# One matmul of 512 tokens per weight tile, instead of two of 256, in the first phase of a convolution and RWKV-7 block

## The chip, the cores and the metric

The kernel runs on one core of a Trainium2 chip. The core has five engines, each with its own queue of instructions that it works off in order: TensorE (PE; its weight loads are listed apart as PEld), VectorE (DVE), ScalarE (ACT), GpSimd (POOL) and SyncE (SP), which issues the DMAs. An instruction may wait for semaphores that other engines or DMAs raise. The metric is the device time of one execution in microseconds (us), the median of three runs.

## The reference, cut to what matters

One layer, 2048 tokens, 1024 channels, float32. A normalised and modulated input `h` goes through one combined projection; a convolution branch and an RWKV-7 branch use its parts, and their merged output goes through further projections.

```python
h = _rmsnorm(x, norm_g[l]) * (1.0 + scale[:, None, :]) + shift[:, None, :]
p = jnp.einsum('bsd,de->bse', h, w_in[l])
c_val, c_gate, c_og, ts, r_og, g_conv, g_rwkv = jnp.split(p, SPLITS, axis=-1)
y_conv = _conv_branch(c_val, c_gate, c_og, conv_k[l], conv_b[l], conv_ln_g[l], conv_ln_b[l], w_conv_out[l])
y_rwkv = _rwkv7_branch(ts, r_og, ...)
m = jax.nn.sigmoid(g_conv) * y_conv + jax.nn.sigmoid(g_rwkv) * y_rwkv
out = jnp.einsum('bsd,de->bse', m, w_out[l])
x = x + gate[:, None, :] * out
...
def step(state, inp):
    r_t, w_t, k_t, v_t, kk_t, b_t = inp
    sk = jnp.einsum('bhvk,bhk->bhv', state, kk_t)
    state = (state * w_t[:, :, None, :] - sk[..., None] * b_t[:, :, None, :]
             + v_t[..., None] * k_t[:, :, None, :])
    return state, jnp.einsum('bhvk,bhk->bhv', state, r_t)
```

The projection has 9344 output columns, 73 tiles of 128 channels. The recurrence (`step`) is serial in the tokens.

## The kernel before

The 2048 tokens are cut into four blocks of 512 (`TB`). The **first phase** makes, for each block, the 73 projection tiles, the convolution and the recurrence, and leaves its results in memory; the **second phase** makes the output projections (tiles `co` and `ro`, then `pout`) and the final norm.

A projection tile (`mm3k`, lines 183 to 193) is a sum over 8 blocks of depth and three products: weights and inputs are split into a high and a low part (`w_hi`, `w_lo`, `h_hi`, `h_lo`) in a rounded 32-bit format, and high x high, high x low and low x high are added in one PSUM tile. Each product is `ms` matmuls over 512 / `ms` tokens; `ms` is `MS` in the first phase and `MS2` in the second. The PSUM tiles `ps_main` come from the pool `pm` with two buffers (line 234), so a projection cannot begin before the last reader of the one two before it is done.

The recurrence runs for 16 heads in four **groups** of two pairs of heads (`group`, `pair`). Before a group can run, each of its pairs needs its projections of k, r and v (`shifted`, lines 410 to 424: ScalarE scales the tile, VectorE adds the previous token's share at L420 and L422, and the small copy at L424 writes `carry`, which is the tile's last reader), the decay (matmuls L452 to L458 with the small weights `wl`, then eight running sums on VectorE at L463, one for each chunk of 64 tokens), head sums (L490), products of keys and queries (L522, masked on VectorE at L524), transposes (L537, L553), and a triangular inversion on GpSimd (L591, L593) with transfers on both sides. Then eight **chunks** follow, each a chain: TensorE L665 and L670, VectorE copies X (L673), TensorE L679, VectorE makes uv (L681), TensorE L685, VectorE updates the state S (L690), and the next chunk's L665 reads S. L650 gives the previous chunk's output. After the last chunk come the group's statistics (L707 to L716) and transposes (L721).

The convolution has 31 taps of 512 tokens on VectorE (L756), 0.75 us each. The projections of the convolution and of the gates (`project`, L730) depend on nothing in the recurrence, so they can stand anywhere between its links.

The order of the instructions in each engine's queue is not the order of the code. A scheduler orders the program when it is built, by its own estimate of how long each instruction takes and by priorities (`high_priority` puts a few ahead). At run time nothing is reordered between the engines' instructions: what stands first in a queue and waits holds up what is behind it.

Of the kernel before, what the change touches and what calls it, by code (L numbers as in the profile page):

```python
# [41 lines left out]
OE, LE, CE = 0, 0, 1  # L42
WLL = 1
TRE = 1
MS, MS2 = 2, 1
WB = 6
KEPT = ("in",)
def lplan(t):
# [1085 lines left out]
```

## Time and profile before

| | |
|---|---|
| median of 3 runs | 3144.74 us (3140.74 to 3146.39) |
| span of the profiled execution | 3131.2 us |
| TensorE's granted clock, mean over the span | 0.981 |
| matmuls of L192 with 256 columns | 4608 for each of the three products, 285 ns each |
| matmuls of L192 with 512 columns (second phase) | 192 or 128 a group of rows, 398 to 421 ns each |
| convolution taps (L756) on VectorE | 697.9 us busy |
| GpSimd's inversion (L591, L593) | 179.8 and 191.9 us busy |
| DMA | 638.42 MB, 204 GB/s over the span |

The profiled span is one execution, from its first instruction to its last, and lies 13.5 us under the median of the runs. Matmuls are pipelined: a row's duration is longer than the distance to the next one's start, and it is that distance which is the rate. In a timeline row stand the start, the duration, engine, line, operation, output and inputs, the shape, and how many instructions were merged; brackets give the idle time before and what ended it. A 32-bit matmul that is not in the rounded format is carried out as two, so four L665 rows in the trace are two in the program.

### The profile page before, as it was taken

The numbers are of one execution on the slowest core, as the hardware profiler recorded it, in microseconds if no ns is written. First come the engines' busy times: TensorE is split into PE (matmuls) and PEld (weight loads), VectorE is DVE, ScalarE is ACT, GpSimd is POOL, SyncE is SP. The second block draws the span as 40 slices with busy tenths as digits, with TensorE's granted clock in tenths as the row PEclk, the third lists the DMA queues.
The fourth block names the chain that finished last, engine by engine and source line by source line (L and its number), as shares of the span: only waits on it lengthen the run. The fifth ranks groups of instructions, "written<-read, shape, count | busy, mean of one in ns | idle before, by whom it ended". The sixth has DMA issues, their size and how long they took to land.

```text
span 3131.2 us, 64840 instructions
## 1 busy us (share of the span) xinstructions
PE 2990.4 (96%) x25672; PEld 2808.5 (90%) x25672; DVE 2169.9 (69%) x4326; ACT 1045.9 (33%) x1887; POOL 1125.1 (36%) x1692
## 2 busy tenths in 40 slices
PE   6799998999999999999999999999999999699998
PEld 5789998999999999999999999999999988487888
DVE  6686877676767665867667586758598455977643
ACT  4424333333323242423142324132332223343421
POOL 3354545424342424141313235326256014643100
PEclk9899999999999999999999999999999999899999
DMA  8665758563747476545546557636457657756554
GB/s 300 215 240 191 259 199 275 195 235 126 256 141 244 150 244 216 190 156 182 178 164 194 186 193 243 198 130 214 137 166 262 215 174 264 261 198 232 189 185 158
DMA packets 343328, 638.42 MB, mean 204 GB/s; under 512 B 133424, under 2 KB 152176, under 8 KB 343024
## 3 DMA queue, kind: packets, MB, share of 16 engines
q1 hardware_dynamic: 343024, 634.27, 60.4%
q8 instruction: 202, 3.31, 0.4%
q14 instruction: 102, 0.84, 0.1%
HBM read 462.10 MB, written 170.92 MB: 202 GB/s over the span
## 4 chain that ended last, share of the span: by engine, by line
PE 71%; DVE 10%; DMA 9%; POOL 4%; issue 2%; SPq 2%; ACT 2%; DVEq 0%; POOLq 0%; ACTq 0%
PE ps_main L192 50%; PE aux L522 3%; PE xo L679 2%; PE xo L650 2%; PE xo L670 2%; DMA w_st<-w_in_t 2%; PE xo L665 2%; PE xo L685 2%; PE pout L1055 1%; POOL TT L593 1%; PE pout L1056 1%; PE pout L1054 1%; POOL itmp L591 1%; DVE acc L756 1%; DMA w_gr<-grow_d 1%
## 5 line engine op out<-in xcount | busy, mean ns | idle before, releaser
L192 PE MATMUL ps_main<-h_hi,w_hi 128*128 128x256 f32 x4608 | 954.9, 285 | 23.1 <-ACT w_hi L175 19.7
L192 PE MATMUL ps_main<-h_hi,w_lo 128*128 128x256 f32 x4608 | 959.1, 285 | 8.1 <-POOL w_lo L177 6.6
L192 PE MATMUL ps_main<-h_lo,w_hi 128*128 128x256 f32 x4608 | 959.0, 285 | 0.0
L192 PEld LDWEIGHTS ps_main<-h_hi,w_hi 128*128 128x128 f32 x4608 | 718.8, 190 | 33.6 <-ACT w_hi L175 20.8
L192 PEld LDWEIGHTS ps_main<-h_hi,w_lo 128*128 128x128 f32 x4608 | 717.2, 189 | 17.9 <-POOL w_lo L177 8.2
L192 PEld LDWEIGHTS ps_main<-h_lo,w_hi 128*128 128x128 f32 x4608 | 717.7, 189 | 6.8 <-issue 0.5
L756 DVE SCALAR_TENSOR_TENSOR acc<-u,ck,acc 128x512 f32<-128x512 f32 x928 | 697.9, 752 | 20.4
L175 ACT CAST w_hi<-w_st 128x1024 fp32r<-128x1024 f32 x135 | 141.5, 1048 | 327.7 <-DMA w_st<-w_in_t 120.8
L591 POOL TENSOR_TENSOR itmp<-La,TT 128x126 f32<-128x126 f32 (+22 forms) x496 | 179.8, 363 | 137.4 <-DMA La<-dA 102.1
L690 DVE SCALAR_TENSOR_TENSOR S<-xo,pe,Se 64x64 f32<-64x64 f32 x512 | 144.8, 283 | 108.4 <-PE xo L685 99.1
L593 POOL TENSOR_TENSOR TT<-TT,itmp 128x126 f32<-128x126 f32 (+22 forms) x496 | 191.9, 387 | 36.0
L177 DVE TENSOR_TENSOR w_lo<-w_st,w_hi 128x1024 fp32r<-128x1024 f32 x88 | 117.8, 1339 | 110.0 <-PE ps_main L192 53.7
L660 ACT ACTIVATE Se<-S,pe 128x128 f32<-128x128 f32 x256 | 89.1, 394 | 232.7 <-DVE S L690 232.3
L177 POOL TENSOR_TENSOR w_lo<-w_st,w_hi 128x1024 fp32r<-128x1024 f32 x47 | 112.5, 2394 | 136.2 <-ACT w_hi L175 83.5
L545 POOL TENSOR_TENSOR vv<-rk,vv 128x512 f32<-128x512 f32 x32 | 43.2, 1350 | 324.4 <-ACT rk L544 324.4
L681 DVE TENSOR_TENSOR uv<-xo,rn 64x256 f32<-64x256 f32 x128 | 53.9, 421 | 129.7 <-PE xo L679 128.7
L522 PE MATMUL aux<-KR,BKz 128*128 128x128 f32 x1024 | 139.9, 282 | 2.8 <-DVE As L524 2.1
L522 PEld LDWEIGHTS aux<-KR,BKz 128*128 128x128 f32 x1024 | 126.2, 194 | 5.7 <-DVE As L524 2.4
L524 DVE TENSOR_TENSOR As<-aux,maskA 128x512 f32<-128x512 f32 x128 | 86.8, 687 | 52.8 <-PE aux L522 51.9
L673 DVE COPY X<-xo 64x256 f32<-64x256 f32 x128 | 53.6, 419 | 89.5 <-PE xo L670 88.6
L652 ACT COPY uv<-xo 64x256 f32<-64x256 f32 x128 | 46.8, 365 | 175.7 <-PE xo L650 175.2
L665 PE MATMUL xo<-S,KR 128*128 128x128 f32 x512 | 96.4, 280 | 6.9 <-DVE S L690 6.7
(294 smaller groups left out, 5464.1 us busy)
## 6 DMA issues: line engine op xcount, KB each, us to landing
w_hi<-kh_in SPq DMA_DIRECT2D x219, 512.0 KB, 3.8
w_lo<-kl_in SPq DMA_DIRECT2D x219, 512.0 KB, 4.9
w_st<-w_in_t SPq DMA_DIRECT2D x73, 512.0 KB, 4.4
kh_in<-w_hi SPq DMA_DIRECT2D x71, 512.0 KB, 2.9
kl_in<-w_lo SPq DMA_DIRECT2D x71, 512.0 KB, 4.3
w_st<-w_ro_t SPq DMA_DIRECT2D x32, 512.0 KB, 3.9
w_st<-w_co_t SPq DMA_DIRECT2D x32, 512.0 KB, 3.5
w_hi<-kh_o SPq DMA_DIRECT2D x32, 512.0 KB, 3.6
```

Source lines behind the costliest of these rows:

```text
L175: nc.scalar.copy(hi, st)
L177: lo_eng.tensor_tensor(out=lo, in0=st, in1=hi.bitcast(F32), op=ALU.subtract)
L192: nc.tensor.matmul(ps[:, qs], ww[:, k, :], aa[k][:, qs], start=(k == 0 and t == 0 and q == 0), stop=(k == KT - 1 and t == 2 and q == ms - ...
L522: nc.tensor.matmul(pA[:, c // 2, es], BKz[:, hh, cc, es], KR[:, cc, es], start=(c == 0), stop=(c == 3), skip_group_check=True)
L524: nc.vector.tensor_tensor(out=Asb[:, hh, c4 * 4:c4 * 4 + 4, :].rearrange("p (a e) n -> p a (e n)", e=2), in0=pA, in1=flat(maskA).unsqueeze ...
L591: nc.gpsimd.tensor_tensor(out=tmp[:, :ni, :nt], in0=La[:, j:j + 1, j + 1:].broadcast_to([P, ni, nt]), in1=TT[:, :ni, j:j + 1].broadcast_to ...
L593: nc.gpsimd.tensor_tensor(out=TT[:, :ni, j + 1:], in0=TT[:, :ni, j + 1:], in1=tmp[:, :ni, :nt], op=ALU.add)
L650: nc.tensor.matmul(xo[vr, q, hs], As[q][:, hh, c, rc], uv[:, c, q, hs], start=False, stop=(q == 1 and hh == 1), skip_group_check=True)
L660: nc.scalar.mul(Se[:, q, :], Sg[:, q, :], R[q]["pe"][:, c:c + 1])
L665: nc.tensor.matmul(xo[:, q, :], R[q]["KR"][:, cc, es], Sg[:, q, :], start=(q == 0), stop=False, skip_group_check=True)
L690: nc.vector.scalar_tensor_tensor(out=Sg[hs, q, hs], in0=xo[hs, 2 + q, hs], scalar=R[q]["pe"][hs, c:c + 1], in1=Se[hs, q, hs], op0=ALU.mult ...
L756: nc.vector.scalar_tensor_tensor(out=acc if i + 1 < HALO else yj, in0=u[:, i:i + TB], scalar=ck[:, j, i:i + 1], in1=acc, op0=ALU.mult, op1 ...
```

## The change

One constant: each product of a projection tile in the first phase is one matmul over all 512 tokens.

```diff
 TRE = 1
-MS, MS2 = 2, 1
+MS, MS2 = 1, 1
 WB = 6
```

In `mm3k` the loop over `q` then runs once, with all of `ps` and of the input tile. The first phase has 292 tiles (73 in four blocks), so 292 x 24 = 7008 pairs of matmuls become single ones, and as many weight loads go. No operation of another engine is added or removed. Since the scheduler orders the program anew, the change moves instructions on all engines. It does so most where one group of the recurrence ends and the next is prepared. The rows below are from the second block, where the second group (state `S_423`) ends and the third (`S_425`) begins.

On TensorE, before, at the last chunks of the group: the rows L192 are projections, two halves each, and between the last chunk's X and uv steps (L679) and those around it stand some ten of them.

```order
L192 MATMUL ps_main<-h_hi,w_lo 128x256 x2
L192 MATMUL ps_main<-h_hi,w_hi 128x256 x2
L192 MATMUL ps_main<-h_lo,w_hi 128x256 x2
L679 MATMUL xo<-X,As 64x64 x4
L665 MATMUL xo<-S_425,KR 128x128 x2
L670 MATMUL xo<-uv,As 64x64 x4
L192 MATMUL ps_main<-h_hi,w_lo 128x256 x2
L192 MATMUL ps_main<-h_hi,w_hi 128x256 x2
```

On TensorE, in the changed kernel, the same boundary:

```order
L192 MATMUL ps_main<-h_hi,w_lo 128x512
L679 MATMUL xo<-X,As 64x64 x4
L685 MATMUL xo<-uv,tk 128x128 x2
L665 MATMUL xo<-S_423,KR 128x128 x2
L670 MATMUL xo<-uv,As 64x64 x4
L650 MATMUL xo<-uv,As 64x64 x4
L679 MATMUL xo<-X,As 64x64 x4
L665 MATMUL xo<-S_425,KR 128x128 x2
L670 MATMUL xo<-uv,As 64x64 x4
L685 MATMUL xo<-uv,tk 128x128 x2
L452 MATMUL aux<-lw,wl 128x512
L453 MATMUL aux<-lw,wlo 128x512
```

Two chunks' links have no projection between them, and the next group's decay matmuls (L452 to L458) follow at once. The queue goes on, up to the next projection:

```order
L457 MATMUL aux<-la,wl 128x512
L458 MATMUL aux<-la,wlo 128x512
L650 MATMUL xo<-uv,As 64x64 x4
L490 MATMUL aux<-bones,sq 64x2 x8
L452 MATMUL aux<-lw,wl 128x512
L453 MATMUL aux<-lw,wlo 128x512
L457 MATMUL aux<-la,wl 128x512
L458 MATMUL aux<-la,wlo 128x512
L192 MATMUL ps_main<-h_hi,w_hi 128x512
```

Both pairs' decay matmuls now stand within a few rows of each other, with nothing of the projections around them; before, they stood further up and apart.

On VectorE, before, around the evacuation of the tiles r and v (L420 to L424) of the next group's second pair:

```order
L681 TENSOR_TENSOR uv<-xo,rn 64x256
L420 SCALAR_TENSOR_TENSOR r<-ps_main,v,t_12946 128x511
L422 SCALAR_TENSOR_TENSOR r<-carry,v,t_12946 128x1
L690 SCALAR_TENSOR_TENSOR S_423<-xo,pe,Se 64x64 x4
L424 COPY carry<-ps_main 128x1
L510 SCALAR_TENSOR_TENSOR rk<-r,hrk,ta 128x512
L420 SCALAR_TENSOR_TENSOR vv<-ps_main,v,t_13036 128x511
L422 SCALAR_TENSOR_TENSOR vv<-carry,v,t_13036 128x1
L673 COPY X<-xo 64x256
L424 COPY carry<-ps_main 128x1
```

On VectorE, in the changed kernel, between the last update of S_423 (with eight scans L463 right behind it) and the carry copy of the next group's first v tile:

```order
L493 TENSOR_SCALAR rn<-aux 128x8
L496 SCALAR_TENSOR_TENSOR y<-ta,k 128x512
L707 TENSOR_REDUCE gst<-uv 128x16
L494 RECIPROCAL rn<-rn 128x8
L483 SCALAR_TENSOR_TENSOR KR<-k,v,E_11274 128x4x64 x2
L497 SCALAR_TENSOR_TENSOR BK<-y,hkk,E_11277 128x4x128
L708 TENSOR_SCALAR gst<-gst 128x16
L463 SCALAR_TENSOR_TENSOR M<-one,M 128x64 x8
L510 SCALAR_TENSOR_TENSOR rk<-r,hrk,ta 128x512
L420 SCALAR_TENSOR_TENSOR vv<-ps_main,v,t_11466 128x511
L422 SCALAR_TENSOR_TENSOR vv<-carry,v,t_11466 128x1
L424 COPY carry<-ps_main 128x1
```

Before, the next group's tiles were evacuated between the links of the running recurrence; now the first v tile stands behind two sets of scans and the preparation of the pair, after the recurrence's end.

## The prediction

> **What bounds the kernel now.** First the page: the span, TensorE's share, the granted clock by slices, and the chain of work that ended last.
>
> ```profile
> span 3131.2 us, 64840 instructions
> PE 2990.4 (96%) x25672; PEld 2808.5 (90%) x25672; DVE 2169.9 (69%) x4326; ACT 1045.9 (33%) x1887; POOL 1125.1 (36%) x1692
> ...
> PE 71%; DVE 10%; DMA 9%; POOL 4%; issue 2%; SPq 2%; ACT 2%; DVEq 0%; POOLq 0%; ACTq 0%
> ```
>
> TensorE is busy 2990 of 3131 us and carries 71% of the chain, so the kernel runs at the rate at which matmuls stream, and the 141 us of idle are what is left of all waits. The question is what the change does to the rate, and what it does to the waits.
>
> Next the timeline of TensorE in a dense stretch of the first phase, where each row is two halves of one weight tile, and through one interruption:
>
> ```profile
> 800.12 0.40 PE L192 MATMUL ps_main<-h_lo,w_hi 128*128 128x256 f32 x2
> ...
> 804.83 0.40 PE L192 MATMUL ps_main<-h_hi,w_hi 128*128 128x256 f32 x2
> 805.07 0.60 PE L721 MATMUL late<-ident,uv 128*128 128x128 f32 x4
> 805.42 0.48 PE L192 MATMUL ps_main<-h_lo,w_hi 128*128 128x256 f32 x2
> 805.75 0.40 PE L192 MATMUL ps_main<-h_hi,w_lo 128*128 128x256 f32 x2
> ```
>
> From 800.12 to 804.83 there are 20 rows, so a pair takes 4.71 / 20 = 235.5 ns. The first pair after a small matmul takes 805.75 - 805.42 = 0.33 us, 0.095 more. The same at 512 columns, from the second phase, where the recurrence's last steps stand between projections:
>
> ```profile
> 2552.53 0.60 PE L665 MATMUL xo<-S,KR 128*128 128x128 f32 x4
> 2553.06 0.67 PE L670 MATMUL xo<-uv,As 64*64 64x64 f32 x8
> 2553.66 0.68 PE L650 MATMUL xo<-uv,As 128*64 128x64 f32 x8
> 2554.27 0.50 PE L192 MATMUL ps_main<-o_lo,w_hi 128*128 128x512 f32 x1
> ...
> 2556.01 0.40 PE L192 MATMUL ps_main<-o_lo,w_hi 128*128 128x512 f32 x1
> ...
> 2559.51 0.39 PE L192 MATMUL ps_main<-o_lo,w_hi 128*128 128x512 f32 x1
> 2559.83 0.68 PE L679 MATMUL xo<-X,As 64*64 64x64 f32 x8
> 2560.43 0.50 PE L192 MATMUL ps_main<-o_hi,w_lo 128*128 128x512 f32 x1
> 2560.77 0.39 PE L192 MATMUL ps_main<-o_lo,w_hi 128*128 128x512 f32 x1
> ...
> 2563.34 0.60 PE L685 MATMUL xo<-uv,tk 128*128 128x128 f32 x4
> 2563.70 0.48 PE L192 MATMUL ps_main<-o_hi,w_hi 128*128 128x512 f32 x1
> ```
>
> From 2556.01 to 2559.51 there are 15 matmuls: 233.3 ns each. After an interruption the first takes 0.34, again 0.1 more. The small matmuls of one chunk of the recurrence occupy TensorE for 0.53 + 0.60 + 0.61 (L665, L670, L650) + 0.60 (L679) + 0.36 (L685) = 2.70 us when projections stand between them.
>
> Such a chunk has a latency of its own, which shows once in the trace, where the order leaves its steps bare:
>
> ```profile
> 2486.86 0.60 PE L685 MATMUL xo<-uv,tk 128*128 128x128 f32 x4
> ...
> 2488.76 1.03 PE L665 MATMUL xo<-S,KR 128*128 128x128 f32 x4 [1.30 <-DVE S L690]
> ...
> 2491.52 1.11 PE L679 MATMUL xo<-X,As 64*64 64x64 f32 x8
> ...
> 2493.16 1.22 PE L685 MATMUL xo<-uv,tk 128*128 128x128 f32 x4 [0.52 <-DVE uv L681]
> ...
> 2495.46 0.63 PE L192 MATMUL ps_main<-o_hi,w_lo 128*128 128x512 f32 x1
> ...
> 2495.88 0.63 PE L192 MATMUL ps_main<-o_hi,w_hi 128*128 128x512 f32 x1
> ```
>
> From L685 to L685 it takes 6.30 us, 3.6 more than TensorE's own 2.70: the steps wait in turn for VectorE (S, X, uv). And behind it the projections come every 0.42 us instead of 0.233: the clock is granted at half.
>
> **The rate.** The change merges 7008 pairs (292 weight tiles of the first phase x 8 blocks of depth x 3 products). 7008 x (235.5 - 233.3 ns) = -15 us. The order has 701 entries into projections (or other 32-bit rounded matmuls) from small matmuls before, and 485 now: 216 x 0.095 = -20 us. Together -35 us, about 1%, and nothing hides them, since TensorE is the bound there.
>
> The Trainium skill ("TensorE: Matmul & The Clock Gate", section "Back-to-back issue gap") gives about 131 ns for a sustained matmul of 512 columns. By that a pair of 235.5 would become 131 and the change would bring -0.7 ms; the row at 233.3 ns, in this kernel with these operands, speaks against it.
>
> **The order.** This is where I expect the loss. The order is made anew, and at 13 of the 16 group boundaries TensorE's queue now has the recurrence's last steps bare, and behind them both pairs' decay matmuls (L452 to L458) of the next group, six rows apart; before, the two never stood closer than 24 rows, with projections between. Links of the recurrence (L665 to L679, L679 to L685, L685 to the next L665) with no projection in them: 4 before, 55 now (group boundaries, where another group's L665 stands in the link, counted as one link). That is about 4 for each of the 13 places, as in the place shown above. The projections that used to fill them are spent earlier, some 22 rows to a link where there were 12.
>
> What the next projection then waits for stands on VectorE. Both buffers of ps_main hold projections (v of the next group's first pair, k of its second), and the next one, r, needs the buffer that v's last reader, the carry copy at L424, gives back. VectorE has ahead of it what the last listing of the change shows (groups: busy us, mean ns of one, idle before):
>
> ```profile
> L463 DVE TENSOR_TENSOR_SCAN M<-one,M 128x64 f32<-128x64 f32 x256 | 82.7, 386 | 7.9 <-ACT M L455 7.4
> ...
> L510 DVE SCALAR_TENSOR_TENSOR rk<-r,hrk,ta 128x512 f32<-128x512 f32 x32 | 37.7, 1178 | 0.2
> ...
> L483 DVE SCALAR_TENSOR_TENSOR KR<-k,v,E 128x256 f32<-128x256 f32 x64 | 32.4, 515 | 0.2
> ...
> L497 DVE SCALAR_TENSOR_TENSOR BK<-y,hkk,E 128x512 f32<-128x512 f32 x32 | 27.8, 867 | 1.2
> ...
> L496 DVE SCALAR_TENSOR_TENSOR y<-ta,k 128x512 f32<-128x512 f32 x32 | 24.1, 755 | 0.0
> ...
> L420 DVE SCALAR_TENSOR_TENSOR vv<-ps_main,v,t 128x511 f32<-128x511 f32 x31 | 23.2, 747 | 29.6 <-ACT t L418 15.7 <-issue 8.2 <-POOL s_lo L271 3.5
> ...
> L707 DVE TENSOR_REDUCE gst<-uv 128x16 f32<-128x1024 f32 x16 | 19.5, 1220 | 6.0 <-ACT uv L652 5.6
> ```
>
> 16 scans x 0.386 + 0.755 (y) + 1.220 (gst) + 2 x 0.515 (KR) + 0.867 (BK) + 1.178 (rk) + 0.747 (vv) = 12.0 us, the small ones left out. None of it is new work, but before it was spread among the taps while TensorE had projections of its own.
>
> One place, from the last projection to the next: L679 to L685 1.64 (2493.16 - 2491.52); a bare chunk 6.30; S and on, 1.9 (2488.76 - 2486.86); VectorE 12.0: together 21.8 us. TensorE's own work in it is 0.60 + 0.36 + 2.70 + 8 decay matmuls x 0.233 = 5.5. So 16 us are lost, and 13 x 16 = **+210 us**. From below: if both sets of scans ran ahead, 6.2 less, and if only the bare links cost, 9.84 - 3.7 = 6 us, 13 x 6 = 78. From above, waits for ScalarE and GpSimd in the same row of steps, 20 us: 260. I take 210, since the scans need the decay matmuls, which stand behind the bare links on TensorE.
>
> After the next projections a second thin stretch follows in the order (L522, L721, L537, L553, L338 with hardly a projection), where VectorE's masks come ahead of the next evacuation:
>
> ```profile
> L524 DVE TENSOR_TENSOR As<-aux,maskA 128x512 f32<-128x512 f32 x128 | 86.8, 687 | 52.8 <-PE aux L522 51.9
> ```
>
> 4 x 0.687 = 2.7 us with TensorE's small matmuls running beside; between 0 and 6 us each I take 3, as the masks take: 13 x 3 = +39 us.
>
> **The clock.** The windows of two stretches (length, then busy us and instructions of TensorE's matmuls and weight loads, VectorE, ScalarE and GpSimd, then the granted clock, the DMA share and GB/s):
>
> ```profile
> 700.00:1000.00 300.00, 297.75 (x2826) 286.26 (x2825) 209.49 (x452) 96.02 (x184) 110.57 (x199) 1.00 0.59 193
> ...
> 2700.00:2800.00 100.00, 80.94 (x349) 63.82 (x350) 78.29 (x87) 39.25 (x54) 55.95 (x36) 0.88 0.59 197
> ```
>
> With TensorE filled the granted clock is 1.00; with 19 us idle in 100 it is 0.88, 12 us of clock. That is 0.63 us for a us of idle, or 10 us for one of the 13 places; the bare chunk above cost the projections behind it only six matmuls at 0.2 extra, 1.3. I take 5: 13 x 5 = +65 us (17 to 130). The Trainium skill ("TensorE: Matmul & The Clock Gate", section "What's actually happening") has it that an idle window of about 3.4 us halves the clock until a busy window has passed; an estimate by it is half of one to two windows, 1.7 to 3.4 us a place or 22 to 44 us, and the sum would be 3380 to 3402. The half-rate rows at 2495.46 agree with it in kind.
>
> **The sum.** 3131 - 35 + 210 + 39 + 65 = 3410 us for the span. The median of the runs, 3144.7, lies 13.5 above the profiled span, so 3424; I say **3420**. The work beside TensorE stays the same: VectorE, ScalarE, GpSimd and the DMAs do what they did, VectorE at 69%.
>
> **Rivals.**
> *The order does not bite, the rate decides* (faster): 3131 - 35 + 13.5 = 3110. For it: TensorE bounds at 96%, and in the stretch 700 to 1000 idles 2 us in 300. It decides if a place loses under 35 / 13 = 2.7 us; against it stands the bare chunk, which alone lost 3.6. 5%.
> *Only the bare links cost*, because VectorE has its scans behind it when TensorE comes: 3131 - 35 + 78 + 17 + 20 + 13.5 = 3225. 12%.
> *It bites harder*: 20 us a place, 6 in the second stretch, 10 of clock: 3131 - 35 + 13 x 36 + 13.5 = 3578. 6%.
> *The change does not do what it says*: it does, the order has 128x512 in phase one throughout; with loss and gain equal the time would stay within 0.2% (6 us, about what a measurement of this kernel can tell): 1%.
> My forecast holds 76%, 3330 to 3505 with the bounds of its terms. The range down to 3225 takes in half of the second rival. Faster 6%, same 2%, slower 92%.
>
> **What would show it.** Right: projections at 128x512 with 230 to 235 ns between starts; L424 (carry) as the releaser of L192's waits, some 100 us in all where it hardly shows now; about 13 stretches of 15 to 35 us with hardly a projection; a granted clock around 0.93 over the span; TensorE's share well below 96%; VectorE's busy time the same. Wrong: no such stretches and a span near 3100, then the steps ran ahead; or stretches ended by another releaser (a weight's DMA, GpSimd's inversion), then the place is right and the mechanism is not. If the projections themselves came faster than 230 ns, my rate is wrong.

## The result, and the profile after

| | median of 4 runs | lowest to highest | span of the profiled execution | TensorE's granted clock |
|---|---|---|---|---|
| before | 3142.74 us | 3137.01 to 3146.39 | 3131.2 us | 0.981 |
| after | 3418.11 us | 3403.50 to 3421.14 | 3415.8 us | 0.931 |

The ratio is 1.0869, with a 95% interval of 1.0844 to 1.0894: 273 us slower, and the forecast was 3420. Differences of medians below are ratios times 3142.7, since each set of runs has its own runs of before beside it.

The changed kernel's page, in the same order as before (span; busy time, share and instructions of each engine; the chain that ended last):

```profile
span 3415.8 us, 50909 instructions
...
PE 3056.6 (89%) x18664; PEld 2504.4 (73%) x18664; DVE 2239.0 (66%) x4326; ACT 1039.5 (30%) x1887; POOL 1125.2 (33%) x1692
...
PE   6899897989898989898989898989879999579998
...
PE 67%; DVE 13%; DMA 8%; POOL 4%; issue 4%; ACT 3%; SPq 1%; DVEq 0%; ACTq 0%; POOLq 0%
```

TensorE issues 7008 matmuls fewer and yet is busy 66 us longer, and idle for 359 us (3415.8 - 3056.6) where it was for 141. In the row of 40 slices (busy tenths of TensorE) nearly every other slice from the fifth on is an 8 or less: a hole that comes back with a period of two slices, some 170 us. What ends the holes is in the view of waits (TensorE's product, what it waited for; us in all, times, the longest) and in the group of the projections' first product (busy us, mean ns; idle before it), in the changed kernel and, below it, before:

```profile
PE ps_main L192 <- DVE carry L424: 143.4, 22, 11.2
```

```profile
L192 PE MATMUL ps_main<-h_hi,w_hi 128*128 128x512 f32 x2304 | 945.8, 411 | 159.2 <-DVE carry L424 143.4
```

```profile
L192 PE MATMUL ps_main<-h_hi,w_hi 128*128 128x256 f32 x4608 | 954.9, 285 | 23.1 <-ACT w_hi L175 19.7 <-DVE carry L424 2.5 <-DMA w_hi<-kh_in 0.5
```

One copy of 128 numbers on VectorE, 0.16 us long, releases 143 us of TensorE's waiting, where it released 2.5 us before. One of the holes in full, TensorE first (start, duration, instruction, idle before it and its releaser):

```profile
1043.24 0.39 PE L192 MATMUL ps_main<-h_hi,w_lo 128*128 128x512 f32 x1
1043.56 0.68 PE L679 MATMUL xo<-X,As 64*64 64x64 f32 x8
1044.75 0.71 PE L685 MATMUL xo<-uv,tk 128*128 128x128 f32 x4 [0.52 <-DVE uv L681]
1046.31 1.03 PE L665 MATMUL xo<-S,KR 128*128 128x128 f32 x4 [0.85 <-DVE S L690]
...
1050.34 0.71 PE L685 MATMUL xo<-uv,tk 128*128 128x128 f32 x4
1051.50 0.50 PE L452 MATMUL aux<-lw,wl 128*128 128x512 f32 x1 [0.45 <-ACT tk L554]
...
1056.65 0.63 PE L458 MATMUL aux<-la,wlo 128*128 128x512 f32 x1
1068.02 0.80 PE L192 MATMUL ps_main<-h_hi,w_hi 128*128 128x512 f32 x1 [10.74 <-DVE carry L424]
1068.61 0.63 PE L192 MATMUL ps_main<-h_lo,w_hi 128*128 128x512 f32 x1
```

From 1043.24 to 1068.02 TensorE has no projection. First the last links of the recurrence run bare, from 1043.56 to 1051; then the next group's decay matmuls, up to 1057; then nothing for 10.74 us. VectorE in the same hole:

```profile
1053.73 2.08 DVE L463 TENSOR_TENSOR_SCAN M<-one,M 128x64 f32<-128x64 f32 x8 [1.39 <-ACT M L455]
...
1057.76 1.92 DVE L483 SCALAR_TENSOR_TENSOR KR<-k,v,E 128x256 f32<-128x256 f32 x2
...
1060.60 4.51 DVE L463 TENSOR_TENSOR_SCAN M<-one,M 128x64 f32<-128x64 f32 x8
1065.03 0.72 DVE L510 SCALAR_TENSOR_TENSOR rk<-r,hrk,ta 128x512 f32<-128x512 f32 x1
1065.79 0.75 DVE L420 SCALAR_TENSOR_TENSOR vv<-ps_main,v,t 128x511 f32<-128x511 f32 x1
1066.45 1.32 DVE L422 SCALAR_TENSOR_TENSOR vv<-carry,v,t 128x1 f32<-128x1 f32 x1
1067.80 0.16 DVE L424 COPY carry<-ps_main 128x1 f32<-128x1 f32 x1
```

VectorE comes free of the recurrence when the decay values arrive (1053.73), works through both pairs' scans and what follows them, and reaches the copy at 1067.80, with hardly a gap: 14.2 us. There are 13 such holes between 527 and 2555 us: more than 15 us without a projection, and each ended by the carry copy. Between 155 and 2600 us the trace of before has no stretch of 10 us without one. Their windows, the first, two from the middle and the last, and the sum of all 13 (length, then busy us and instructions of TensorE's matmuls, its weight loads, VectorE, ScalarE and GpSimd, the granted clock, the DMA share and GB/s):

```profile
527.40:550.70 23.30, 9.43 (x82) 6.67 (x80) 16.57 (x39) 11.82 (x22) 11.11 (x13) 0.78 0.35 127
...
1043.30:1068.00 24.70, 10.72 (x90) 7.33 (x88) 18.09 (x40) 10.95 (x22) 9.63 (x12) 0.76 0.15 53
1210.00:1234.70 24.70, 10.39 (x91) 7.13 (x89) 18.08 (x40) 10.96 (x22) 9.61 (x12) 0.77 0.15 54
...
2510.90:2555.10 44.20, 24.97 (x155) 19.15 (x153) 40.13 (x84) 12.87 (x28) 9.43 (x14) 0.61 0.13 38
sum 352.20, PE 170.09 PEld 123.40 DVE 254.76 ACT 144.55 POOL 139.54; mean PE 13.08 PEld 9.49 DVE 19.60 ACT 11.12 POOL 10.73
```

352.2 us in 13 holes, 27.1 each, of which TensorE is idle 182 (352.2 - 170.1), 14.0 each.

### The profile page after: what moved, and what is told of

It reads as the page before. It is cut to its first block, busy times and chain, and to the rows that moved or that the text cites. A ratio compares the mean times of both kernels' runs of the same rounds, so it can differ in the third digit from the quotient of the medians.

```text
span 3415.8 us, 50909 instructions
## 1 busy us (share of the span) xinstructions
PE 3056.6 (89%) x18664; PEld 2504.4 (73%) x18664; DVE 2239.0 (66%) x4326; ACT 1039.5 (30%) x1887; POOL 1125.2 (33%) x1692
## 4 chain that ended last, share of the span: by engine, by line
PE 67%; DVE 13%; DMA 8%; POOL 4%; issue 4%; ACT 3%; SPq 1%; DVEq 0%; POOLq 0%; ACTq 0%
PE ps_main L192 46%; PE aux L522 3%; DVE M L463 3%; PE xo L670 2%; PE xo L679 2%; DMA w_st<-w_in_t 2%; PE xo L650 2%; PE xo L665 2%; PE pout L1054 2%; PE pout L1056 2%; PE pout L1055 2%; PE xo L685 2%; DMA w_gr<-grow_d 1%; POOL TT L593 1%; POOL itmp L591 1%
## 5 line engine op out<-in xcount | busy, mean ns | idle before, releaser
L192 PE MATMUL ps_main<-h_hi,w_hi 128*128 128x512 f32 x2304 | 945.8, 411 | 159.2 <-DVE carry L424 143.4
L192 PE MATMUL ps_main<-h_hi,w_lo 128*128 128x512 f32 x2304 | 934.5, 406 | 9.1 <-DMA w_lo<-kl_in 4.6
L192 PE MATMUL ps_main<-h_lo,w_hi 128*128 128x512 f32 x2304 | 936.1, 407 | 0.3 <-DVE h_lo L351 0.3
L192 PEld LDWEIGHTS ps_main<-h_hi,w_hi 128*128 128x128 f32 x2304 | 447.8, 194 | 266.4 <-DVE carry L424 154.1
L192 PEld LDWEIGHTS ps_main<-h_hi,w_lo 128*128 128x128 f32 x2304 | 446.7, 194 | 111.2 <-POOL w_lo L177 6.8
L192 PEld LDWEIGHTS ps_main<-h_lo,w_hi 128*128 128x128 f32 x2304 | 447.9, 194 | 93.2 <-DVE h_lo L351 0.7
L690 DVE SCALAR_TENSOR_TENSOR S<-xo,pe,Se 64x64 f32<-64x64 f32 x512 | 144.8, 283 | 140.6 <-PE xo L685 130.2
L593 POOL TENSOR_TENSOR TT<-TT,itmp 128x126 f32<-128x126 f32 (+22 forms) x496 | 186.0, 375 | 36.5
L450 POOL TENSOR_TENSOR wlo<-wf,wl 64x128 fp32r<-64x128 f32 x64 | 34.2, 535 | 362.8 <-ACT wl L447 318.8
L418 ACT ACTIVATE t<-ps_main,mu 128x512 f32<-128x512 f32 x96 | 65.9, 687 | 237.7 <-PE ps_main L192 226.2
L522 PE MATMUL aux<-KR,BKz 128*128 128x128 f32 x1024 | 133.0, 280 | 3.9 <-ACT ta L460 3.9
```

What stands on the lines that cost most here:

```text
L192: nc.tensor.matmul(ps[:, qs], ww[:, k, :], aa[k][:, qs], start=(k == 0 and t == 0 and q == 0), stop=(k == KT - 1 and t == 2 and q == ms - ...
L522: nc.tensor.matmul(pA[:, c // 2, es], BKz[:, hh, cc, es], KR[:, cc, es], start=(c == 0), stop=(c == 3), skip_group_check=True)
L593: nc.gpsimd.tensor_tensor(out=TT[:, :ni, j + 1:], in0=TT[:, :ni, j + 1:], in1=tmp[:, :ni, :nt], op=ALU.add)
L690: nc.vector.scalar_tensor_tensor(out=Sg[hs, q, hs], in0=xo[hs, 2 + q, hs], scalar=R[q]["pe"][hs, c:c + 1], in1=Se[hs, q, hs], op0=ALU.mult ...
```

## The experiments

Three questions: is it the matmul or the order, is it the carry copy or what stands around it, and on what does the length of a hole depend. Where a kernel was changed after its instructions had been put in order, the order on every engine stays as it was and only the named instructions differ.

### The matmul apart from the order

The order of before, and in it each pair of neighbouring halves joined to one matmul of 512 columns (6682 of the 7008 pairs; in the others something stands between the halves). The core of it:

```diff
+                    new[held] = copy.replace(a, ins=(wide(a.ins[0]), a.ins[1]), outs=(wide(oa),), ...)
...
     with tile.TileContext(nc, schedule_with_timeline_sim=True) as tc:
         hybrid_block(tc, *args, out)
+    merge_halves(nc)
```

> The program of the kernel before in its own order on every engine; after the ordering, 6682 of the 7008 pairs of halves that stand next to each other on TensorE are made one matmul of 512 columns each. Theory (the loss is in the new order): only the rate changes, 6682 x 2.2 ns = -15 us, so about 3128 us, between 3110 and 3140, clock near 0.98, waits for the carry copy as few as before. Rival (the longer matmul itself costs: the recurrence's steps wait behind longer pieces of work, or the wide matmuls run worse): near the changed kernel's 3418, certainly above 3250.

Measured: **3120.30 us**, ratio 0.9925 (0.9899 to 0.9952), that is 24 us faster than before. The matmuls of the change in the order of before bring a gain; nothing of the 273 us is in the matmul itself.

The other way round, the changed kernel's order with each matmul cut into two neighbouring halves:

```diff
+                new.append(copy.replace(i, ins=(half(i.ins[0], 0), i.ins[1]), outs=(half(i.outs[0], 0),), stop_tensor_calc=False, ...))
+                new.append(copy.replace(i, ins=(half(i.ins[0], 1), i.ins[1]), outs=(half(i.outs[0], 1),), start_tensor_calc=False, ...))
```

> The program of the changed kernel in its own order on every engine; after the ordering, each of the 7008 matmuls of 512 columns is made two neighbouring ones of 256. Theory (the order): 3418 + 15 = 3433 us, between 3415 and 3455, with some 140 us of waits for the carry copy. Rival (the longer matmul itself): back near 3143.

Measured: **3444.73 us**, ratio 1.0957 (1.0926 to 1.0988), 28 us more than the changed kernel. With the matmuls of before the loss stays whole, its waits for the carry copy are 140.5 us, and the two runs put about the same price on the matmul, 24 and 28 us, each known to some 10 us. The page of the first of the two kernels, for the comparison with the changed one:

```profile
span 3117.9 us, 51484 instructions
...
PE 2968.1 (95%) x18990; PEld 2468.6 (79%) x18990; DVE 2175.9 (70%) x4326; ACT 1046.6 (34%) x1887; POOL 1128.0 (36%) x1692
```

These two kernels do the same work with nearly the same matmuls in two orders. The spans differ by 297.9 us: TensorE is idle for 359.2 us against 149.8, which is 209 more, and busy 88 us more (3056.6 - 2968.1). The holes go with the order: in that of before the joined kernel has none, and the carry copy ends 2.6 us of idle.

```profile
L192 PE MATMUL ps_main<-h_hi,w_hi 128*128 128x512 f32 x2208 | 885.2, 401 | 26.1 <-ACT w_hi L175 22.4 <-DVE carry L424 2.6 <-DMA w_hi<-kh_in 0.7
```

The same joining with the second phase also put in order by halves (`MS2 = 2`; the lines are against the kernel before):

```diff
-MS, MS2 = 2, 1
+MS, MS2 = 2, 2
```

> The program ordered with halves of 256 in the first phase and also in the second, and the neighbouring halves of both merged into products of 512 columns after the ordering. If the gain of a finer grain for the ordering carries over to the second phase: 3095 to 3115 us. If the second phase has no order to gain: within 6 of the 3120 us of the run that merged the first phase alone.

Measured: 3120.47 us, ratio 0.9937 (0.9916 to 0.9959). No gain beyond the first phase; the simpler version stands as the faster kernel, at 3120.

### The carry copy

The wait's releaser is the carry copy, so the plain cure is to put the evacuation ahead of the scans. First by priority:

```diff
+        with tc.high_priority(HP):
             nc.vector.scalar_tensor_tensor(out=dst[:, 1:], in0=ps[:, 0:TB - 1], scalar=mu, in1=t1[:, 1:],
...
             nc.vector.tensor_copy(carry[:, mi:mi + 1], ps[:, TB - 1:TB])
```

> The changed kernel with the four lines of VectorE that read a k, r or v tile out of PSUM (L420 to L424) raised in priority, so that the order puts them ahead of the scans and of the pair's preparation. Theory (the next projection waits for the carry copy behind 12 us of VectorE work at 13 places): the wait of L192 for carry falls from 143 us to under 40, and the time by 100 to 220 us, to 3200 to 3320; what is left over 3143 are the bare links and the clock. Rival (the stretch is bound by the recurrence's end and the decay matmuls, and carry only comes last by a little): the wait moves to another releaser and the time stays above 3370.

Measured: **3432.42 us**, ratio 1.0921. A miss: the wait is still there (the copy is line 425 in this kernel),

```profile
PE ps_main L192 <- DVE carry L425: 147.2, 22, 12.1
```

and the copy's place in VectorE's queue did not change. The raised lines could not pass L510: `vv` is written into r's buffer (`VVT = "r"`), r's last reader is L510, and L510 was not raised and stands behind the scans. So `vv` got a buffer of its own:

```diff
-HXB = 7
+HXB = 6
...
-VVT, SHT, RKT, RHT, YT = "r", "sh", "k", "sh", "y"
+VVT, SHT, RKT, RHT, YT = "vv", "sh", "k", "sh", "y"
```

> The changed kernel, with vv in a buffer of its own instead of r's (the free space for it comes from one x tile fewer). In the changed kernel the evacuation of the vv product (L420 to L424) stands behind L510, the last reader of r, and so behind the 16 scans; with its own buffer it stands ahead of them, and the wait of L192 for that carry copy (143.4 us in 22 waits) has lost its cause. Theory 1 (the copy's place in VectorE's queue is itself the price): 13 stretches shorter by about 11 us each, so 3250 to 3310 us. Theory 2 (projections have run out for the recurrence to run under, and the next evacuation, r of the next pair, is held by the same scans): the wait moves to that evacuation, the stretches stay, and the time is within 25 of 3418 us.

Measured: **3428.84 us**, ratio 1.0910 (1.0887 to 1.0933). Theory 2: the time is that of the changed kernel or a little more. The waits, and VectorE in the hole that is the same place as the one above:

```profile
PE ps_main L192 <- DVE carry L424: 147.0, 21, 11.4
```

```profile
1077.84 4.51 DVE L463 TENSOR_TENSOR_SCAN M<-one,M 128x64 f32<-128x64 f32 x8
1082.28 0.72 DVE L510 SCALAR_TENSOR_TENSOR rk<-r,hrk,ta 128x512 f32<-128x512 f32 x1
1083.04 0.75 DVE L420 SCALAR_TENSOR_TENSOR r<-ps_main,v,t 128x511 f32<-128x511 f32 x1
1083.70 1.31 DVE L422 SCALAR_TENSOR_TENSOR r<-carry,v,t 128x1 f32<-128x1 f32 x1
1085.05 0.16 DVE L424 COPY carry<-ps_main 128x1 f32<-128x1 f32 x1
```

The evacuation that ends the hole is now that of r, not of vv: the projections got one tile further and then stood before the same scans. The releaser that the view of waits names is the last link; taking it away alone gives nothing, since the next tile is held by the same work. It is held by the same L510, too: the pool `e1` has one buffer for r (line 241), so r of the next pair must wait until L510 has read the one before. A kernel in which neither tile waits for L510 was not run, and so it stays open whether the hole would then close. That the projections had run out, the other half of theory 2, this run doesn't show.

### What the length of a hole depends on

The scans L463 made shorter, in the changed kernel's order:

```diff
+            if getattr(i, "is_tensor_tensor_scan", False):
+                i = copy.replace(i, ins=tuple(one_col(p) for p in i.ins), outs=tuple(one_col(p) for p in i.outs))
```

> The changed kernel in its own order, with the running sums of the decay (L463) cut to the first token of each chunk: 256 scans of 1 column for 64, so the sums themselves are left out. Theory (VectorE's row of 12 us is the path in the thin stretches, the scans 6 us of it): 13 x 16 x (0.386 - 0.1) = 60 us less, 3340 to 3395. Rival (VectorE's row runs beside something longer there): within 15 us of 3418.

Measured: **3390.92 us**, ratio 1.0790 (1.0770 to 1.0810), 25 us less. That lies in the expected range only because the range was wide: 60 us had been worked out, and the cut is smaller. One scan (ns: lowest, median, highest) in the changed kernel and in this one:

```profile
L463 DVE TENSOR_TENSOR_SCAN M<-one,M x256: 231/261/2279, 75.8 to 2551.9; 128x64 f32<-128x64 f32 x128
```

```profile
L463 DVE TENSOR_TENSOR_SCAN M<-one,M x256: 100/149/1873, 76.7 to 2529.5; 128x1 f32<-128x1 f32 x128
```

16 x (261 - 149 ns) = 1.8 us a hole, or 23 us for 13. In the trace the 13 holes are 21 us shorter in sum (352 and 331 us). So VectorE's work in a hole is paid about one for one, as far as a difference known to some 10 us can say.

The same cut at the state update L690:

```diff
+            if x.startswith("xo") and t in ("S0", "S1", "S2", "S3"):
+                i = copy.replace(i, ins=tuple(one_col(p) for p in i.ins), outs=tuple(one_col(p) for p in i.outs))
```

> The changed kernel's own order, with the state update L690 cut to the first of its 64 columns (the rest of the state update is left out). Each link's update is then shorter by about 0.6 us (four of 0.28 us become four of about 0.13). Theory (the links of the recurrence stand bare in the thin stretches, some 40 updates): 15 to 45 us less, 3373 to 3403 us. Rival (the VectorE work of the next pair sets the end of those stretches whatever the links do): within 10 of 3418 us.

Measured: 3412.10 us, ratio 1.0861 (1.0839 to 1.0884), which is not to be told from the changed kernel's 1.0869. The rival had named this time, but the run decides nothing, because the cut was too small:

```profile
L690 DVE SCALAR_TENSOR_TENSOR S<-xo,pe,Se x512: 196/218/228, 241.5 to 2882.1; 64x1 f32<-64x1 f32 x171
```

An update of one column takes 218 ns where 64 take 284, so four of them are 0.26 us shorter and not 0.6; 40 updates would be 10 us.

Both cuts in the order of before, as a control:

> A control: the order of before, with both shortenings at once, the scans L463 cut to their first column and the state update to its first column (running sums and most of the state update are left out). Theory (in the order of before this work runs under projections): 0 to 20 us less than before, 3122 to 3142 us. Rival (shorter work pays in any order as it did in the changed one): 45 to 70 us less, 3072 to 3097 us.

Measured: 3131.58 us, ratio 0.9961 (0.9945 to 0.9976), 12 us less, as the theory had it: about half of what the scans alone brought in the changed order. Most of this work, but not all of it, has cover in the order of before.

A link made longer is the clearer test than one made shorter. One reduction of a mask, read by nothing, ahead of each of the 128 state updates, in the changed order and in that of before with the joined halves:

```diff
+                if tuple(m.split("_")[0] for m in at) in ahead and at not in seen:
+                    seen.add(at)
+                    new.append(copy.replace(red, ..., ins=(copy.replace(mask, ap=[list(mask.ap[0]), [0, 4], [1, 256]], ...),), ...))
...
+    pad(nc, {("S%d" % g, "xo") for g in range(4)})
```

> The changed kernel's own order, with one reduction of 1024 columns of the mask (some 1.2 us by L707's rows) put on VectorE ahead of each of the 128 state updates L690; nothing else reads it. Theory (about 40 updates stand bare, in 13 stretches; the others run under projections): 40 x 1.2 = 48 us more, and some for the clock: 3455 to 3490 us. Rival (the update is on the path at every chunk): 128 x 1.2 = 154 us more, 3555 to 3590 us.

> The same reductions ahead of the state updates in the order of before with merged halves (3120 us). Theory (in that order 18 gaps between links are bare where the changed one has 70, so a quarter as many updates): 12 us more, 3125 to 3145 us. Rival (the order of before has no more slack at its links than the changed one): as much more as in the changed kernel, 3165 us or above.

```profile
L690 DVE TENSOR_REDUCE carry<-maskA x128: 1198/1221/1224, 243.3 to 2943.4; 128x4 f32<-128x1024 f32 x128
```

Measured: changed order **3470.20 us**, ratio 1.1035 (1.1012 to 1.1057), 52 us more; order of before 3146.78 us, ratio 1.0000 (0.9988 to 1.0013), 24 us more than without the reductions. 52 / 1.22 is as much as 43 updates of 128 on the path, where the theory had 40. In the order of before it is 19, against the 10 expected: the rival falls (it wanted as many there as here), but the median lies just above the 3145 that the theory allowed.

The same at the start of a pair, one reduction of 3072 columns ahead of the first L483 of each pair:

```diff
+    pad(nc, {("KR", "k")})
```

> The changed kernel's own order, with one reduction of 3072 columns (some 3.6 us) put on VectorE ahead of the first L483 of each of the 32 pairs. Theory (VectorE's work at the start of a pair stands ahead of the evacuation that TensorE waits for, one for one, in 13 stretches, and once more ahead of the second one): 13 x 3.6 = 47 us more for the first alone, 94 with the second, and some for the clock: 3465 to 3540 us. Rival (that work is under cover): within 15 of 3418 us.

> The same 32 reductions in the order of before with merged halves (3120 us). Theory (there the start of a pair runs under projections): 0 to 35 us more, 3120 to 3155 us. Rival (every order has this work on its path): 32 x 3.6 = 115 us more or as much as in the changed kernel, 3215 us or above.

```profile
L483 DVE TENSOR_REDUCE carry<-maskA x32: 3302/3346/3354, 78.8 to 2669.7; 128x12 f32<-128x3072 f32 x32
```

```profile
PE ps_main L192 <- DVE carry L424: 213.5, 29, 13.4
```

Measured: changed order **3515.08 us**, ratio 1.1178 (1.1161 to 1.1195), 97 us more: 97 / 3.35 is as much as 29 of the 32, and the wait for the carry copy alone grew from 143.4 to 213.5 us, by 70. In the order of before 3181.22 us, ratio 1.0112 (1.0097 to 1.0128), 59 us more, so 18 of 32. There the expectation of 35 at most missed: the order of before hides less of this work than I thought, though it hides more than the changed one, where 38 us more are paid.

## Why the prediction was right, step by step

**The mechanism.** The loss is the order, shown from both sides by the two kernels that keep one and change the other (3120 and 3445). Its place is where the prediction had it: the last links bare, the decay matmuls behind them, then both pairs' scans and the rest on VectorE ahead of the carry copy. There are 13 holes of the 13 forecast, 143 us of waits on L424 where some 100 were expected, and both parts of a hole are on the path: longer links cost 43 updates' worth, longer starts 29 of 32 (19 and 18 in the order of before). One thing the prediction didn't say, and the runs showed: the carry copy is only the last releaser. With its cause removed another evacuation takes its place, at no gain.

**The sum.** For the span the prediction had 3131 - 35 + 210 + 39 + 65 = 3410, and 3415.8 came. The single terms were less good than the sum, and their errors cancelled, so a total within 6 us is luck in part. For the median the prediction added the 13.5 us by which it lay above the profiled span before; here it lies 2.3 above.

| term | predicted | measured |
|---|---|---|
| the rate | -15 | -24 by the joined halves in the order of before, -28 by the split ones in the changed order |
| fewer switches | -20 | not measured apart; the traces have 701 entries into projections from small matmuls before and in the joined kernel, 485 in the changed one, so this term is part of the last row |
| the hole | 13 x 21.8 us long, 13 x 16 = 210 lost | 13 x 27.1 long; TensorE idle for 182 us in all, and busy some 55 longer |
| the second thin stretch | 13 x 3 = 39 | 12 stretches, 17 us of idle in all |
| the clock behind the holes | 13 x 5 = 65 | some 2.3 each, 30 in all |
| order, switches, second stretch and clock | 294 | 298, of which 209 idle and 88 busy |

The 55 us are an estimate from two traces: at the mean busy time that each kind of matmul has in the joined kernel, those in the 13 holes would take 115 us, and they take 170. Hole, second stretch and clock then make 284 us. What fewer switches saved, and what is lost elsewhere, was not measured.

*The hole.* The one shown takes 24.8 us where the prediction had 21.8. Ahead of the scans it is 10.5 us (1043.24 to 1053.73, bare links and the way to the decay values), against 1.64 + 6.30 + 1.9 = 9.8. Of the 6.30 the prediction had put 3.6 down to waits for VectorE. In part it was the clock: the rows there last 1.03 to 1.22 us, and the same rows between projections 0.60 to 0.68. The term that was mis-sized is VectorE's: 14.2 us from the first scan to the carry copy, where the sum of the means had 12.0. The operations that were summed take 12.6 here (their rows overlap a little). The small ones that were left out take 2.3, and 1.32 of it is one update of a single column (L422); the last section shows why. And three holes are longer than all others, 35.0, 36.5 and 44.2 us, with 20 to 25 us of TensorE's own work in them; they lift the mean to 27.1.

*The second stretch.* The sum of the twelve windows behind the holes, where TensorE has small matmuls of the next group:

```profile
1077.50:1086.30 8.80, 6.75 (x49) 5.21 (x47) 4.85 (x10) 6.68 (x14) 1.27 (x1) 1.00 0.62 204
...
sum 117.90, PE 100.49 PEld 84.93 DVE 72.94 ACT 77.39 POOL 21.52; mean PE 8.37 PEld 7.08 DVE 6.08 ACT 6.45 POOL 1.79
```

17.4 us of idle in twelve, 1.4 each: the masks run beside TensorE's small matmuls more than the 3 us allowed for.

*The clock.* The 7 us behind three of the holes:

```profile
1068.00:1075.00 7.00, 6.98 (x20) 5.60 (x21) 3.20 (x13) 2.64 (x4) 1.05 (x1) 0.64 0.01 4
1234.70:1241.70 7.00, 7.00 (x19) 5.56 (x20) 3.20 (x13) 2.62 (x4) 1.07 (x1) 0.61 0.00 0
...
2555.10:2562.10 7.00, 7.00 (x18) 5.48 (x19) 2.98 (x13) 2.43 (x3) 1.90 (x1) 0.57 0.00 0
```

TensorE is full, and the clock is granted at 0.57 to 0.79 over the 13 windows: 7 x (1 - 0.67) is about 2.3 us each, 30 in all. The 5 had been chosen from between 1.3 and 10 and was too much for the stretch behind a hole. The range of 22 to 44 us that the prediction had worked out as an estimate from the Trainium skill ("TensorE: Matmul & The Clock Gate", section "What's actually happening") holds the 30. Most of the rest of the 88 us of longer busy time lies in the holes themselves (the 55 above), where the granted clock is 0.61 to 0.78 in the four windows shown and small matmuls stand alone, with their whole duration as busy time; the two were not parted.

*The rate.* Neighbouring starts in a dense stretch of the order of before, joined:

```profile
800.00 0.39 PE L192 MATMUL ps_main<-h_lo,w_hi 128*128 128x512 f32 x1
...
805.95 0.39 PE L192 MATMUL ps_main<-h_hi,w_hi 128*128 128x512 f32 x1
```

26 matmuls in 5.95 us, 228.8 ns each. Over all such distances at the full granted clock the median is 230.0 ns, in the joined kernel and in the changed one, and a pair of halves takes 236.0 before. The prediction's 233.3 came from 15 matmuls of the second phase and was too slow, and the 230 that it had named as the sign of a wrong rate is just reached: a pair gains 6 ns, not 2.2. That would be 40 us for 6682 pairs, and 24 arrived. In part the rest shows as waits: TensorE is idle for 149.8 us in the joined kernel, 9 more than before.

**The other signs.** The granted clock is 0.931 (0.93 forecast), TensorE's share 89%, the projections are 128x512 throughout. VectorE's busy time was to stay the same and rose by 69 us, from 2169.9 to 2239.0, with the same 4326 instructions (2175.9 in the joined kernel, so the order does it); the last section shows where 50 of the 69 us lie.

**The rivals.** That the order doesn't bite, and that only the bare links cost, ask for 3110 and 3225. The first comes near the time of the kernel that has the change's matmuls without its order (3120). Its 3110 counted 20 us for fewer switches, which that kernel doesn't have, and too little for the rate; its condition, that the order doesn't bite, was false.

## What to carry to other kernels

Where a scheduler orders the program by its own estimates, changing an instruction's size changes two things, and they can be measured apart: order with the old pieces, and join them after the ordering. Here the matmul alone is worth 24 us, and the order that it brought cost 298. A wait's releaser in a profile is the last of a chain, so before moving it, ask which instruction would be the next to hold the same engine: here the same scans held the next tile, and two attempts at the copy gave nothing. And when a test shortens an instruction, look up first what is left of it at the smallest size.

## What the hardware showed that was not expected

Some of VectorE's operations take longer while GpSimd is at work. GpSimd in the hole shown above:

```profile
1061.25 1.31 POOL L503 TENSOR_TENSOR BK<-ta,E 128x512 f32<-128x512 f32 x1
1062.52 1.89 POOL L709 TENSOR_TENSOR uv<-uv,gst 128x1024 f32<-128x1024 f32 x1
...
1066.49 1.27 POOL L271 TENSOR_TENSOR s_lo<-rk,rh 128x512 fp32r<-128x512 f32 x1 [0.38 <-ACT rh L542]
```

The second set of eight scans lasts 4.51 us beside the first two of these; the first set, beside two short operations of GpSimd only (L450, some 0.5 us each), 2.08. The update of one column (L422, 128x1) lasts 1.32 us beside the third, from 1066.45 to 1067.77, and GpSimd's own from 1066.49 to 1067.76: they end together. Over the whole program, this update and the scans, each in the group of before and of the changed kernel (busy us, mean ns):

```profile
L422 DVE SCALAR_TENSOR_TENSOR vv<-carry,v,t 128x1 f32<-128x1 f32 x32 | 9.2, 289 | 0.0
```

```profile
L422 DVE SCALAR_TENSOR_TENSOR vv<-carry,v,t 128x1 f32<-128x1 f32 x32 | 24.6, 770 | 0.0
```

```profile
L463 DVE TENSOR_TENSOR_SCAN M<-one,M 128x64 f32<-128x64 f32 x256 | 82.7, 386 | 7.9 <-ACT M L455 7.4
```

```profile
L463 DVE TENSOR_TENSOR_SCAN M<-one,M 128x64 f32<-128x64 f32 x256 | 104.0, 474 | 25.7 <-ACT M L455 25.7
```

With L483 (32.4 and 45.5 us busy) these make 50 of the 69 us by which VectorE's busy time rose. In the changed kernel's trace 191 of VectorE's operations last over 0.3 us longer than the median of their group (groups of eight or more, 4236 operations). All 191 run beside an instruction of GpSimd, though only 1487 of the 4236 do, and 190 of them read two tensors from SBUF. No operation with a tensor in PSUM is among them. The state update reads `xo` from there (lowest, median and highest time in ns),

```profile
L690 DVE SCALAR_TENSOR_TENSOR S<-xo,pe,Se x512: 262/284/294, 239.5 to 2885.3; 64x64 f32<-64x64 f32 x171
```

and stays within 10 ns above its median, although 143 of the 512 run beside GpSimd. So do the convolution's taps, whose sum `acc` is in PSUM: 483 of 928 run beside GpSimd, and the longest takes 758 ns where the median is 756.

The Trainium skill ("SBUF — State Buffer", section "SBUF: two separate sides") has it that VectorE, in an operation with two inputs in SBUF, and GpSimd share one pair of ports, which is held for the whole of an instruction while the other engine's waits; the 191 operations and the ends at 1067.77 and 1067.76 agree. It was not tested by a run of its own. The run with short scans shifted it: there GpSimd's L709 meets L510 in place of a scan, and L510 takes 2.47 us where it takes 0.72 in the hole above. By these rows some 5.5 us of VectorE's 14.2 in the hole are waiting for GpSimd (3.5 in the scans, against their median of 0.26 each; 1.0 in L483; 1.1 in L422, whose median for k and r is 0.21), and the order that puts both engines' work into the same hole pays for that too. The other surprise was the floor of a small operation: cut from 64 columns to one, a state update still took 218 of its 284 ns, and a scan 149 of 261.
